# A mean square summed by TensorE, and the first modulation weights loaded in two halves

## The chip, the core and the metric

The kernel runs on one core of a Trainium2 chip. Its time is the device time of one execution in microseconds; before the change the median of three runs is 1152.08 us (1148.12 to 1154.47). The core has five engines with instruction queues of their own: TensorE (PE; its weight loads are listed as PEld), VectorE (DVE), ScalarE (ACT), GpSimd (POOL) and SyncE (SP), which here issues the DMA transfers. Each queue is worked off in order, so an instruction that waits holds up all that stand behind it in its queue.

## The reference, cut to what matters

Two transformer blocks over 512 tokens of width 1024, in float32. The change is at the entry of the first block:

```python
mod = silu(c) @ w_mod + b_mod                     # w_mod: 1024 x 3072
shift, scale, gate = split(mod, 3)
u = x * rsqrt(mean(x*x, axis=-1) + 1e-6) * norm_w * (1 + scale) + shift
p = u @ w_in                                      # and so on: attention, convolution, output
```

## The kernel before, in words

Activations lie transposed: the 1024 features are eight tiles `xs[0..7]` of 128 partitions x 512 tokens. So the mean square of a token is a sum over partitions and tiles, and the factor 1/rms must be the same on all partitions of a column; it is kept as a tile `bs` of 128 x 512 that holds it on every partition.

The first block begins in these steps (`block1`, line 341):

1. SP issues the loads in the order of the program: vectors and a constant, the eight tiles of x, group 0 of `w_mod` (four transfers of 128 x 1024, `mod_load`), two of the eight pieces of `w_start`, group 1 of `w_mod`; the rest as buffers come free (two for `wr`, ten for `modw`).
2. `warm_up` gives TensorE 8 + 20 products of zeros, whose results nobody reads.
3. `norm_bs`: ScalarE squares each tile, VectorE adds the squares up (seven additions), TensorE reduces over partitions with four products by a column of 1/1024, ScalarE takes the root and VectorE the reciprocal of 128 x 4 numbers, TensorE spreads them by four transposes, and ScalarE copies the result into `bs`.
4. `mod_group` multiplies one group of `w_mod` (512 columns) by silu(c): eight products that write 32 partitions each, four of them side by side in the array; ScalarE copies the result from PSUM (`part`); four small products by `sel32` give it in columns (`cols`). `mod_pair` makes shift and scale (`shift`, `A1`) for two feature tiles of it, on VectorE. Groups 0 to 3 serve the tiles 0 to 7, groups 4 and 5 the gate.
5. For each tile j, `apply_mod` makes u: x * bs on VectorE, then scale and shift on ScalarE into a high part, the same into float32, and the low part by a subtraction on VectorE. `w_start[j]` is split the same way into `wh` and `wl`. Then come 18 products (six outputs, three each: high x high, weights x low part, low weights x high): the block of tile j. They accumulate in PSUM over the eight blocks.

One PSUM bank (`pj`) serves the warm-up, the sum of squares and `mod_group` in turn, one (`pv`) the `cols`. The pool `tA` has four buffers. A scheduler puts the instructions of each engine in order when the program is built, from dependencies and its own estimate of times; so instructions of one block may stand among those of another. Behind the eight blocks come the gated products (`glu`), the convolution on VectorE (31 taps for each of four tiles, put off by a low priority), the projections with `w_in`, and q with `w_q` (first piece of it: a tile `wh` too).

Of the kernel before, what the change touches and what calls it, by code (L numbers as in the profile page):

```python
# [16 lines left out]
AF = mybir.ActivationFunctionType  # L17
# [5 lines left out]
P = 128  # L23
S = 512
D = 1024
KT = 8
# [120 lines left out]
def rest(k, src, hi, lo):  # L147
    return k.V.tensor_tensor(out=lo, in0=src, in1=hi.bitcast(F32), op=ALU.subtract)
# [32 lines left out]
def mm3(k, ps, wh, wl, ah, al, first, last):  # L181
    mm = k.T.matmul
    mm(ps, wh, ah, start=first, stop=False)
    mm(ps, wh, al, start=False, stop=False)
    k.mm = mm(ps, wl, ah, start=False, stop=last)
    return k.mm
# [77 lines left out]
def bcast(k, r, n, tag):  # L264
    b = k.t(tag)
    for j in range(n):
        k.T.transpose(b[:, j * P:(j + 1) * P], r[:, j:j + 1].to_broadcast([P, P]), k.ident)
    return b
# [66 lines left out]
MODW = 10  # L335
LATER = 1500
CTX = (0, 2)
WARM = (8, 20, 0)
ZG = (1, 0, 1, 1, 1, 0, 0, 0, 0, 0, 0)

def block1(k, I, st, h1d):
    A, V, T, G, Y = k.A, k.V, k.T, k.G, k.Y
    k.consts("c1", 1408)
    S1 = ExitStack()
    k.open(S1, "S", dict(modw=MODW, bs=1))

# [3 lines left out]
    def warm_up(n):  # L350
        ps = k.t("pj")
        for _ in range(n):
            T.matmul(ps, warm[:, 0:P], warm, start=True, stop=True)

    xs = []
# [8 lines left out]
    cc = k.cal([KT, 32])  # L364
# [2 lines left out]
    A.activation(th[:, 0:1], th[:, 0:1], AF.Sqrt, scale=0.0, bias=k.eps[1e-6])  # L367

    mark = [None] * 3
    warm_up(WARM[0])  # L370
    warm_up(WARM[1])
    shift, A1 = k.cal([2, KT]), k.cal([2, KT])
    gate = k.cal([KT])
    bm1 = k.cal([KT])
# [2 lines left out]
    def mod_load(g, i):  # L377
        t = k.t("modw", [2, S])
        Y.dma_start(out=t, in_=I["w_mod"][g, i])
        return t  # L380

    def mod_group(ts):
        ps = k.t("pj")
        for kt in range(KT):
            q = 32 * (kt % 4)
            T.matmul(ps[q:q + 32, :], cc[:, kt, :], ts[kt // 2][:, kt % 2, :], start=kt < 4, stop=kt >= 4)
        part = k.t("tA")
        A.activation(part, ps, AF.Copy)
        cols = k.t("pv", [4, 2])
        for i in range(4):  # L390
            T.matmul(cols[:, i, :], part[:, i * P:(i + 1) * P], k.sel32[:, 0:2], start=True, stop=True)
        return cols

    def mod_pair(g, ts):
        cols = mod_group(ts)
        for e in range(2):
            j = 2 * g + e
            V.tensor_scalar(out=shift[:, :, j], in0=cols[:, 2 * e, :], scalar1=k.vec("b_mod", j), scalar2=None, op0=ALU.add)
            V.tensor_scalar(out=A1[:, :, j], in0=cols[:, 2 * e + 1, :], scalar1=bm1[:, j:j + 1],
                            scalar2=k.vec("norm_w", j), op0=ALU.add, op1=ALU.mult)  # L400

    def mod_gate(g, ts):
        cols = mod_group(ts)
        V.tensor_tensor(out=gate[:, 4 * g - 16:4 * g - 12], in0=cols[:, :, 0], in1=k.vec("b_mod", 4 * g, 4), op=ALU.add)

    def norm_bs(vals, w, tag):
        ss = SumSq(k, "tA", w)
        for v in vals:
            ss.add(v)
        r = ss.rstd("pj", k.inv1k, 1e-6, k.cal([w // P]))  # L410
        b = bcast(k, r, w // P, "pv")
        bs = k.t(tag, [D] if tag == "modw" else [w])[:, :w]
        mark[1] = A.activation(bs, b[:, :w], AF.Copy)
        return bs

    def apply_mod(x, w, bs, i, j, hi, lo, vec=False):
        t = k.t("tA", [w])
        mark[1] = V.tensor_tensor(out=t, in0=x, in1=bs, op=ALU.mult)
        a_ap, s_ap = A1[:, i, j:j + 1], shift[:, i, j:j + 1]
        A.activation(hi, t, AF.Identity, bias=s_ap, scale=a_ap)  # L420
        if vec:
            V.tensor_scalar(out=t, in0=t, scalar1=a_ap, scalar2=s_ap, op0=ALU.mult, op1=ALU.add)
        else:
            mark[2] = A.activation(t, t, AF.Identity, bias=s_ap, scale=a_ap)
        V.tensor_tensor(out=lo, in0=t, in1=hi.bitcast(F32), op=ALU.subtract)
        return hi, lo

    bs = norm_bs(xs, S, "bs")
    warm_up(WARM[2])
    a0, a1 = k.t("s", [2, S]), k.t("s", [2, S])  # L430
    accs = [a0[:, 0, :], a0[:, 1, :], a1[:, 0, :], a1[:, 1, :], k.t("pt"), k.t("pt")]
    us = []

    mods = [[mod_load(0, i) for i in range(4)]]
    raws = []

    def raw_load(j):
        raw = k.t("wr", [1024])
        Y.dma_start(out=raw[:, :768], in_=I["w_start"][j])
        raws.append(raw)  # L440

    raw_load(0)
    raw_load(1)
    mods.append([mod_load(1, i) for i in range(4)])
    for j in range(KT):
        raw, wh, wl = raws[j], k.t("wh", [1024], F32R), k.t("wl", [1024], F32R)
        A.activation(wh[:, :768], raw[:, :768], AF.Copy)
        if j % 2 == 0:
            mod_pair(j // 2, mods[j // 2])
        u = apply_mod(xs[j], S, bs, 0, j, k.t("U", dt=F32R), k.t("U", dt=F32R))  # L450
        us.append(u)
        rest(k, raw[:, :768], wh[:, :768], wl[:, :768])
        if j + 2 < KT:
            raw_load(j + 2)
        if j % 2 == 0 and j // 2 + 2 < 6:
            mods.append([mod_load(j // 2 + 2, i) for i in range(4)])
        for m in range(6):
            c = slice(m * P, (m + 1) * P)
            mm3(k, accs[m], wh[:, c], wl[:, c], u[0], u[1], j == 0, j == KT - 1)
# [41 lines left out]
    for g in range(4):  # L501
        wh, wl = W1.next()
        for kk in range(2):
            j = 2 * g + kk
            c = slice(kk * S, (kk + 1) * S)
            for t in range(4):
                tt = slice(t * P, (t + 1) * P)
                uh, ul = us[j]
                ps = q_ps[t // 2][:, t % 2, :]
# [18 lines left out]
    for t in (2, 3, 4, 5, 0, 1):  # L528
        ps = k.t("pt", [256])
        for j in range(KT):  # L530
# [3 lines left out]
            o = (t if t < 2 else t - 2) * P  # L534
# [222 lines left out]
    for pr in range(4):  # L757
        for half in range(2):
            i = 2 * pr + half
# [27 lines left out]
    for m in range(KT):  # L787
        ps = k.t(("pj", "pt", "pt", "pv")[m % 4])
# [652 lines left out]
def emit(tc, I, out, dbg=None, stages=("b1", "b2", "ff")):  # L1441
    k = K(tc, dbg)
    nc = tc.nc
    with ExitStack() as st:
        k.open(st, "g", dict(g=1, wr=2, wh=3, wl=2))
        setup(k, I)
        h1d = nc.dram_tensor("h1d", (KT, P, S), F32, kind="Internal").ap()
        k.open(st, "H", dict(xa=6, xb=4, hg=16))
        p1 = ExitStack()
        k.open(p1, "p1", dict(c1=1, U=16, tA=4, kvs=6))  # L1450
        k.open(p1, "p1m", dict(pj=1), PSUM)
        k.open(p1, "p1s", dict(s=2), PSUM)
        k.open(p1, "p1t", dict(pt=2), PSUM)
        k.open(p1, "p1v", dict(pv=1), PSUM)
        if "b1" not in stages:
            k.rest()
        if "b1" in stages:
            nm = block1(k, I, p1, h1d)
        else:
            nm = Norm(k, "norm_mix_g", "hg", "xb")  # L1460
            for j in range(KT):
                x = k.x()
                k.Y.dma_start(out=x, in_=I["xT"][:, j, :])
                k.Y.dma_start(out=h1d[j], in_=x)
                nm.add(j, x)
        p1.close()
        k.nx = 0
        if "b2" in stages:
            k.open(st, "p2a", dict(c2=1, p=6, rk=4, v=2, z=2, bon=3, s8=6, nr=8))
            k.open(st, "p2m", dict(pj=2), PSUM)  # L1470
            k.consts("c2", 1350)
            block2(k, I, nm, h1d, out)
# [94 lines left out]
```

## Time and profile before

| | |
|---|---|
| runs | 1152.08 us median of 3 (1148.12 to 1154.47) |
| profiled execution | 1149.1 us, of which the span is 1147.3 us |
| PE busy | 1084.9 us, 95% |
| DVE busy | 728.2 us, 63% |
| ACT busy | 538.3 us, 47% |
| first matmul of a block of u | 23.32 us |
| last matmul of the eighth block | 72.22 us |
| first matmul of the projection behind them | 78.38 us |

The table's upper part is from the page, its last three rows from the timeline of TensorE. Nearly all instructions are recorded on line 57, a helper, so they are told apart by their tiles: `s<-U,wh` writes the accumulator s from a high part of u (U) and a high part of weights (wh). A product in float32 is recorded as two matmuls, so x16 stands for eight products of `mod_group`; a product of the blocks is recorded as one. The kernel does nothing over and over, so a microsecond at its entry counts once.

### The profile page before, as it was taken

To read this page: it belongs to the slowest core of one execution; us is meant where nothing else is said; L and a number is where in the kernel's file an instruction comes from. 1 tells how busy PE (TensorE), PEld (TensorE's weight loads), DVE (VectorE), ACT (ScalarE), POOL (GpSimd) and SP (SyncE) were. 2 spreads that over 40 slices of the span, in tenths; PEclk is the share of its full clock that TensorE was granted. 3 is DMA by queue.
4 is the path that set the end of the run, shared out by engine and by line. 5 is a ranking of instruction groups with operands and counts; after the bars stand their busy time and mean duration, and the time that the engine had idled before them with its cause. 6 is when DMAs were issued, how large, how long until landed. Compare 5 with 4: busy or idle time off the path is not lost.

```text
span 1147.3 us, 15927 instructions
## 1 busy us (share of the span) xinstructions
PE 1084.9 (95%) x6268; PEld 835.6 (73%) x6268; DVE 728.2 (63%) x1260; ACT 538.3 (47%) x987; POOL 66.9 (6%) x222
## 2 busy tenths in 40 slices
PE   7999989985998899999999898999999999999998
PEld 3668966553686677777768675768888888888887
DVE  3459999986454698888866888657444334334332
ACT  5444546766434366564646575555434133233220
POOL 0000000000001111121111012010000000000000
PEclk8999999997998999999989998999999999999999
DMA  8753221001143211010101221212232233233332
GB/s 304 266 199 96 74 88 38 1 23 32 55 166 105 67 38 56 20 38 19 38 20 52 74 75 37 75 55 84 86 106 92 92 103 99 92 94 107 94 118 85
DMA packets 30603, 96.46 MB, mean 84 GB/s; under 512 B 3392, under 2 KB 4160, under 8 KB 30528
## 3 DMA queue, kind: packets, MB, share of 16 engines
q1 hardware_dynamic: 30528, 95.45, 25.6%
q8 instruction: 49, 0.80, 0.3%
q14 instruction: 26, 0.21, 0.1%
HBM read 91.24 MB, written 4.19 MB: 83 GB/s over the span
## 4 chain that ended last, share of the span: by engine, by line
PE 81%; DVE 7%; ACT 4%; POOL 3%; issue 2%; DMA 2%; SPq 0%; ACTq 0%; DVEq 0%; POOLq 0%
PE pf L57 30%; PE pj L57 23%; PE i L57 7%; PE s L57 7%; PE pt L57 6%; PE pv L57 4%; PE y L57 3%; POOL nr L57 3%; DVE hg L57 2%; ACT p L57 1%; DVE c L57 1%; DVE wl L57 1%; DVE tA L57 1%; ACT wh L57 1%; DMA wr<-w_in 1%
## 5 line engine op out<-in xcount | busy, mean ns | idle before, releaser
L57 ACT ACTIVATE wh<-wr 128x1024 fp32r<-128x1024 f32 (+1 forms) x132 | 137.5, 1042 | 175.7 <-PE pf L57 63.5
L57 DVE TENSOR_TENSOR wl<-wr,wh 128x1024 fp32r<-128x1024 f32 (+1 forms) x132 | 158.6, 1203 | 11.8 <-ACT wh L57 4.5
L57 PE MATMUL pj<-hg,wh 128*128 128x512 f32 x448 | 155.0, 418 | 3.2 <-ACT r L57 1.8
L57 PE MATMUL pf<-A,wh 128*128 128x512 f32 x512 | 157.7, 389 | 0.0
L57 ACT ACTIVATE f<-i 128x512 f16<-128x512 f32 (+1 forms) x132 | 72.0, 597 | 90.6 <-PE i L57 90.5
L57 PEld LDWEIGHTS pf<-A,wh 128*128 128x128 f32 x512 | 96.0, 188 | 19.7
L57 PE MATMUL pf<-A,wl 128*128 128x512 f32 x256 | 99.6, 389 | 0.0
L57 PEld LDWEIGHTS pj<-hg,wh 128*128 128x128 f32 x448 | 81.4, 193 | 20.6 <-issue 2.0
L57 DVE TENSOR_TENSOR x<-x,pf 128x512 f32<-128x512 f32 (+1 forms) x33 | 22.1, 671 | 114.0 <-PE pf L57 114.0
L57 PE MATMUL pj<-hg,wl 128*128 128x512 f32 x224 | 91.0, 406 | 1.5 <-DVE wl L57 1.5
L57 DVE SCALAR_TENSOR_TENSOR hg<-hg,c 128x498 f32<-128x498 f32 (+14 forms) x120 | 84.8, 735 | 0.4
L57 PE MATMUL pf<-ff,wh 128*128 128x512 f32 (+1 forms) x272 | 79.7, 377 | 0.0
L57 PE MATMUL pf<-hg,wh 128*128 128x512 f32 x256 | 78.8, 389 | 0.0
L57 DVE SCALAR_TENSOR_TENSOR fr<-pf,r 128x512 f32<-128x512 f32 x32 | 22.1, 691 | 85.4 <-PE pf L57 82.1
L57 ACT ACTIVATE fr<-fr 128x512 f32<-128x512 f32 x32 | 20.2, 632 | 100.2 <-DVE fr L57 100.2
L57 PEld LDWEIGHTS <-f 128*128 128x128 f16 x720 | 46.0, 100 | 23.6 <-issue 14.3
L57 PE MATMUL i<-f 128*128 128x128 f16 x672 | 55.7, 224 | 5.7 <-DVE f L57 5.3
L57 PEld LDWEIGHTS pf<-ff,wh 128*128 128x128 f32 x272 | 50.1, 188 | 9.4
L57 PE MATMUL pj<-U,wh 128*128 128x512 f32 x160 | 53.3, 410 | 3.4 <-DVE hg L57 3.3
L57 PEld LDWEIGHTS pf<-A,wl 128*128 128x128 f32 x256 | 48.0, 188 | 10.1
L57 PEld LDWEIGHTS pf<-hg,wh 128*128 128x128 f32 x256 | 48.0, 188 | 10.0
L57 PE MATMUL pf<-ff,wl 128*128 128x512 f32 (+1 forms) x136 | 51.2, 376 | 0.0
(302 smaller groups left out, 2123.9 us busy)
## 6 DMA issues: line engine op xcount, KB each, us to landing
wr<-w_ff SPq DMA_DIRECT2D x64, 512.0 KB, 3.5
modw<-w_mod SPq DMA_DIRECT2D x24, 512.0 KB, 7.0
wr<-rw_in SPq DMA_DIRECT2D x20, 512.0 KB, 3.5
wr<-w_out SPq DMA_DIRECT2D x16, 512.0 KB, 3.5
wr<-w_in SPq DMA_DIRECT2D x10, 512.0 KB, 3.5
wr<-w_start SPq DMA_DIRECT2D x8, 384.0 KB, 4.3
x<-xT SPq DMA_DIRECT2D x8, 256.0 KB, 5.2
wr<-w_q SPq DMA_DIRECT2D x4, 512.0 KB, 3.6
```

The lines of the kernel that those rows point to most:

```text
L57: r = f(*a, **kw)
```

## The change

It does two things in `block1`, and sets two constants.

- The sum of squares: a constant 128 x 128 matrix of 1/1024 (`ones`) is multiplied by each square, accumulating over the eight tiles in `pj`. The result is the mean square on every partition. ScalarE takes the root of all 128 x 512 numbers into `bs`, and VectorE the reciprocal of all of them, in place. The seven additions, the four products by a column, the small root and reciprocal, the four transposes and the copy are gone for x; `norm_bs` stays for the context.
- Group 0 of `w_mod` is loaded as two halves of 256 columns (four transfers of 128 x 2 x 256 each), the first before `w_start[0]`, the second between `w_start[0]` and `w_start[1]`. `mod_group` and `mod_pair` take the range of halves, and tile 0 calls the first, tile 1 the second. The other groups stay whole.
- 12 warm-up products in place of 28, and 128 columns more for constants.

```diff
-WARM = (8, 20, 0)
+WARM = 12
...
-    def mod_group(ts):
+    def mod_group(ts, e0=0, e1=2):
         ps = k.t("pj")
+        o = slice(e0 * 256, e1 * 256)
         for kt in range(KT):
             q = 32 * (kt % 4)
-            T.matmul(ps[q:q + 32, :], cc[:, kt, :], ts[kt // 2][:, kt % 2, :], start=kt < 4, stop=kt >= 4)
+            T.matmul(ps[q:q + 32, o], cc[:, kt, :], ts[kt // 2][:, kt % 2, o], start=kt < 4, stop=kt >= 4)
         part = k.t("tA")
-        A.activation(part, ps, AF.Copy)
+        A.activation(part[:, o], ps[:, o], AF.Copy)
         cols = k.t("pv", [4, 2])
-        for i in range(4):
+        for i in range(2 * e0, 2 * e1):
...
-    bs = norm_bs(xs, S, "bs")
-    warm_up(WARM[2])
+    ones = k.cal([P])
+    G.memset(ones, 1.0 / D)
+    ps = k.t("pj")
+    for j in range(KT):
+        sq = k.t("tA")
+        A.activation(sq, xs[j], AF.Square)
+        T.matmul(ps, ones, sq, start=j == 0, stop=j == KT - 1)
+    bs = k.t("bs")
+    A.activation(bs, ps, AF.Sqrt, bias=k.eps[1e-6])
+    V.reciprocal(out=bs, in_=bs)
...
-    mods = [[mod_load(0, i) for i in range(4)]]
+    mods = [[k.t("modw", [2, S]) for i in range(4)]]
+
+    def half_load(e):
+        for i in range(4):
+            Y.dma_start(out=mods[0][i][:, :, e * 256:(e + 1) * 256], in_=I["w_mod"][0, i][:, :, e * 256:(e + 1) * 256])
+    half_load(0)
...
     raw_load(0)
+    half_load(1)
     raw_load(1)
...
-        if j % 2 == 0:
+        if j < 2:
+            mod_pair(0, mods[0], j, j + 1)
+        elif j % 2 == 0:
             mod_pair(j // 2, mods[j // 2])
```

The scheduler also moves instructions, on TensorE at three places. The first is the entry, behind the warm-up; `pj<-modw` are the products of `mod_group`, `pv<-g,tA` its small products, `s` and `pt` the accumulators of the blocks, `c_83` the tile of constants.

```order
-L57 MATMUL pj<-g,tA 128x1 x4
-L57 MATMUL pj<-modw,c_83 32x512
-L57 MATMUL pv<-g,c_83 128x128 x4
-L57 MATMUL pj<-modw,c_83 32x512 x7
-L57 MATMUL pv<-g,tA 128x2 x4
+L57 MATMUL pj<-tA,c_83 128x512 x8
+L57 MATMUL pj<-modw,c_83 32x256 x8
+L57 MATMUL pv<-g,tA 128x2 x2
+L57 MATMUL pj<-modw,c_83 32x256 x8
+L57 MATMUL pv<-g,tA 128x2 x2
 L57 MATMUL s<-U,wh 128x512 x2
 L57 MATMUL pt<-U,wh 128x512 x2
```

Both halves of group 0 stand ahead of the first block, though only tile 1 needs the second. On ScalarE, too, the two copies of `part` stand ahead of the first high part of u.

The second place is TensorE between the blocks of tiles 1 and 2, with groups 1 and 2 of `w_mod`.

```order
 L57 MATMUL pt<-U,wh 128x512 x2
 L57 MATMUL pt<-U,wl 128x512
-L57 MATMUL pj<-modw,c_83 32x512 x6
+L57 MATMUL pj<-modw,c_83 32x512 x4
 L57 MATMUL pv<-g,tA 128x2 x4
-L57 MATMUL pj<-modw,c_83 32x512 x6
+L57 MATMUL pj<-modw,c_83 32x512 x8
 L57 MATMUL s<-U,wh 128x512 x2
 L57 MATMUL pt<-U,wh 128x512 x2
-L57 MATMUL pj<-modw,c_83 32x512 x2
+L57 MATMUL pv<-g,tA 128x2 x4
 L57 MATMUL s<-U,wh 128x512
```

Group 1 was cut into 2 + 6 products and is now cut into 4 + 4; group 2 was 6 + 2 and is whole. Groups 3 and 4 were 5 + 3 each, the latter parts among the first products of tiles 4 and 6; now both are whole and stand between tiles 5 and 6, so that the blocks of tiles 2 to 5 follow one another.

The third place is TensorE behind the block of tile 7, with group 5. First the rows before, then the rows now; `s<-wh,U` are products of q with the first piece of `w_q`, `pj<-U` the first projection.

```order
L57 MATMUL pt<-U,wl 128x512
L57 MATMUL pv<-g,tA 128x2 x4
L57 MATMUL pj<-modw,c_83 32x512 x8
L57 MATMUL pv<-g,tA 128x2 x4
L57 MATMUL pj<-U,wh 128x512 x2
```

```order
L57 MATMUL pt<-U,wl 128x512
L57 MATMUL pv<-g,tA 128x2 x4
L57 MATMUL pj<-modw,c_83 32x512 x8
L57 MATMUL s<-wh,U 128x512 x2
L57 MATMUL pv<-g,tA 128x2 x4
L57 MATMUL pj<-U,wh 128x512 x2
```

Two products of q have come up ahead of the last small products and of the projections; they need the first piece of `w_q`, split by ScalarE. VectorE's queue now has the low part of the first `w_in` piece ahead of the gated products, and the load of `w_q` waits for that. Behind the convolution, about a quarter into the program, the orders before and after are the same.

## Rows read from the trace of the kernel before

**Rows 1.** The page's first part: busy us (share) x instructions of each engine
```profile
PE 1084.9 (95%) x6268; PEld 835.6 (73%) x6268; DVE 728.2 (63%) x1260; ACT 538.3 (47%) x987; POOL 66.9 (6%) x222
```
**Rows 2.** Stretches: length, busy PE, PEld, DVE, ACT, POOL; clock; DMA share, GB/s
```profile
4.70:9.60 4.90, 4.74 (x21) 1.86 (x19) 1.99 (x3) 4.46 (x8) 0.00 (x0) 1.00 0.94 317
9.60:13.00 3.40, 0.00 (x0) 0.02 (x1) 2.85 (x5) 1.85 (x3) 0.00 (x0) 0.80 1.03 413
13.00:15.20 2.20, 1.84 (x8) 1.77 (x8) 0.01 (x1) 0.27 (x1) 0.00 (x0) 0.50 1.02 415
```
**Rows 3.** Timeline of PE, entry: start, us, instruction, [idle before, releaser]
```profile
1.41 8.09 PE L57 MATMUL pj<-bs 128*128 128x512 bf16 x28 [1.41 <-POOL bs L57]
...
15.26 1.89 PE L57 MATMUL pj<-modw,c 128*32 128x512 f32 x2 [0.40 <-issue]
...
18.12 2.06 PE L57 MATMUL pj<-modw,c 128*32 128x512 f32 x14
20.92 1.05 PE L57 MATMUL pv<-g,tA 128*128 128x2 f32 x8 [0.74 <-ACT tA L57]
23.32 0.74 PE L57 MATMUL s<-U,wh 128*128 128x512 f32 x2 [1.35 <-ACT U L57]
...
25.65 0.50 PE L57 MATMUL s<-U,wh 128*128 128x512 f32 x1
```
**Rows 4.** Timeline of ACT, entry
```profile
8.17 3.36 ACT L57 ACTIVATE tA<-x 128x512 f32<-128x512 f32 x5 [0.28 <-DMA x<-xT]
...
20.27 0.60 ACT L57 ACTIVATE tA<-pj 128x512 f32<-128x512 f32 x1 [1.38 <-PE pj L57]
...
22.45 0.81 ACT L57 ACTIVATE U<-tA,c 128x512 fp32r<-128x512 f32 x1 [0.86 <-DVE c L57]
```
**Rows 5.** Timeline of PE, the blocks and behind them
```profile
33.12 1.91 PE L57 MATMUL pj<-modw,c 128*32 128x512 f32 x12
...
51.89 1.06 PE L57 MATMUL pj<-modw,c 128*32 128x512 f32 x6
...
72.22 0.39 PE L57 MATMUL pt<-U,wl 128*128 128x512 f32 x1
73.78 1.05 PE L57 MATMUL pv<-g,tA 128*128 128x2 f32 x8 [1.17 <-ACT tA L57]
...
77.47 1.05 PE L57 MATMUL pv<-g,tA 128*128 128x2 f32 x8 [0.78 <-ACT tA L57]
78.38 0.71 PE L57 MATMUL pj<-U,wh 128*128 128x512 f32 x2
```
**Rows 6.** Stretch behind the blocks, columns as in Rows 2
```profile
78.40:90.00 11.60, 11.60 (x53) 9.64 (x53) 10.85 (x23) 2.40 (x3) 0.00 (x0) 1.00 0.22 73
```
**Rows 7.** Timeline of DVE, entry
```profile
7.40 5.47 DVE L57 TENSOR_TENSOR tA<-tA 128x512 f32<-128x512 f32 x7 [3.77 <-ACT tA L57]
...
18.92 1.29 DVE L57 TENSOR_TENSOR tA<-x,bs 128x512 f32<-128x512 f32 x2 [3.55 <-ACT bs L57]
```
**Rows 8.** Timeline of PE: products of 128 x 512 with a constant matrix in float32
```profile
225.12 2.74 PE L57 MATMUL pj<-hg,c 128*128 128x512 f32 x6
```
**Rows 9.** DVE groups by shape: count | busy us, mean ns | idle before
```profile
L57 DVE RECIPROCAL c<-c 128x8 f32<-128x8 f32 x6 | 1.2, 197 | 3.3 <-ACT AR L57 3.3
...
L57 DVE RECIPROCAL c<-c 128x2 f32<-128x2 f32 x2 | 0.3, 154 | 0.0
```
**Rows 10.** DMA issues between 5.00 and 5.41: count, KB each, us to landing
```profile
x<-xT SPq DMA_DIRECT2D x1, 256.0 KB, 5.9
```
**Rows 11.** Stretches of transfers at the entry, columns as in Rows 2
```profile
2.20:2.60 0.40, 0.40 (x2) 0.15 (x1) 0.00 (x0) 0.00 (x0) 0.00 (x0) 1.00 0.85 234
5.00:6.00 1.00, 0.98 (x5) 0.48 (x5) 0.00 (x0) 0.98 (x2) 0.00 (x0) 1.00 0.91 305
14.00:15.00 1.00, 0.85 (x5) 0.77 (x4) 0.00 (x0) 0.11 (x1) 0.00 (x0) 0.50 1.03 414
```
**Rows 12.** Timeline of ACT: the first piece of w_q
```profile
78.01 1.05 ACT L57 ACTIVATE wh<-wr 128x1024 fp32r<-128x1024 f32 x1
```

More of the change, by code (lines that the diff above doesn't have):

```diff
@@ L342, in block1 @@
     A, V, T, G, Y = k.A, k.V, k.T, k.G, k.Y
-    k.consts("c1", 1408)
+    k.consts("c1", 1536)
     S1 = ExitStack()
@@ L369, in block1 @@
     mark = [None] * 3
-    warm_up(WARM[0])
-    warm_up(WARM[1])
+    warm_up(WARM)
     shift, A1 = k.cal([2, KT]), k.cal([2, KT])
@@ L380, in mod_load, with mod_pair @@
         return t
-    def mod_group(ts):
+    def mod_group(ts, e0=0, e1=2):
         ps = k.t("pj")
+        o = slice(e0 * 256, e1 * 256)
         for kt in range(KT):
             q = 32 * (kt % 4)
-            T.matmul(ps[q:q + 32, :], cc[:, kt, :], ts[kt // 2][:, kt % 2, :], start=kt < 4, stop=kt >= 4)
+            T.matmul(ps[q:q + 32, o], cc[:, kt, :], ts[kt // 2][:, kt % 2, o], start=kt < 4, stop=kt >= 4)
         part = k.t("tA")
-        A.activation(part, ps, AF.Copy)
+        A.activation(part[:, o], ps[:, o], AF.Copy)
         cols = k.t("pv", [4, 2])
-        for i in range(4):
+        for i in range(2 * e0, 2 * e1):
             T.matmul(cols[:, i, :], part[:, i * P:(i + 1) * P], k.sel32[:, 0:2], start=True, stop=True)
         return cols
-    def mod_pair(g, ts):
-        cols = mod_group(ts)
-        for e in range(2):
+    def mod_pair(g, ts, e0=0, e1=2):
+        cols = mod_group(ts, e0, e1)
+        for e in range(e0, e1):
             j = 2 * g + e
```

## The prediction

> **What bounds the kernel now.** The page's first part comes first: TensorE is busy for 1084.9 us of the span, VectorE for 728.2 [rows 1]. So the change is worth what it takes from TensorE's waiting and from TensorE's own work at the entry, and no more. The stretches of the entry are read next, then TensorE's timeline. The reader is to see a hole. The warm-up ends at 9.5 us [rows 3]; until 13.0 TensorE has nothing, because VectorE's seven additions take 5.47 us behind the squares [rows 7]. In that hole the granted clock drops: 1.00 up to 9.60, 0.80 on average up to 13.00, 0.50 after (1.2 instead of 2.4 GHz) [rows 2]. So the first product of group 0, with the transposes queued behind it, runs at the lower clock: 1.89 us for one product, while the seven others then take 2.06 us together [rows 3]. Only after that come the copy of 0.60 us at 20.27, the small products until 21.97, and the first high part of u at 22.45 [rows 3, 4]. The first block starts at 23.32, and its first product with a low part at 25.65 [rows 3]. From there to the last product of the eighth block, at 72.22 [rows 5], TensorE has only short gaps.
>
> **The sum of squares.** Removed from the path: the additions, four column products, the small root and reciprocal, four transposes and the copy. Added: eight products of 128 x 512 by a constant matrix. Three such take 2.74 us elsewhere [rows 8], which is 0.85 us from one to the next and 0.2 us for the last to drain. ScalarE delivers the third square just before 7.9 us and the eighth at 11.53 [rows 4], 0.67 us each, so TensorE is the slower. With twelve warm-up products it is free at about 5.6 (21 of the 28 lie in the 4.90 us from 4.7 on, 0.23 us each; seven or eight came before [rows 2, 3]); by the third square it is at work on the second until 8.2, and six more take it to 13.3, plus the drain 13.5. The pool's four buffers don't slow this: square five needs the first product's buffer, long done. The root of 128 x 512 from PSUM I take as the copy's 0.60 us [rows 4]: 14.1. The reciprocal of 512 columns does not occur. From 2 to 8 columns it grows by 43 ns [rows 9], 7.2 ns a column, so 3.8 us; the floor is a plain pass over 128 x 512, 0.65 us [rows 7]; the ceiling, had those few columns understated the slope by two thirds, is 6.3 us. I take 3.8: `bs` is ready at 17.9, against 18.89 before by the end of its copy (VectorE's first use starts at 18.92 [rows 7]). That alone would win little; what matters is what else is late by then.
>
> **The two halves.** The last tile of x lands at about 11.0 (issued just after 5.0, 5.9 us to landing [rows 10]); transfers keep the order of issue. Group 0's halves come in runs of 1 KB instead of 4 KB. Runs of 4 KB moved at 414 GB/s, the 2 KB runs of x at 305, the first vectors with 1.1 KB at 234 with the engines busy for 0.85 of the time [rows 11]. For 1 KB I take 250 GB/s, near the last. The bounds: 414, if only the start of the program made the earlier rates low; and 200, by a line through the times of a run at 2 and 4 KB (16 engines: 107 and 158 ns, so 82 ns at 1 KB). A half of 1.05 MB takes 4.2 us (2.5 to 5.2). So the first half lands at 15.2, `w_start[0]` 0.95 us later at 16.2, the second half at 20.4, `w_start[1]` at 21.3, and the first two tiles of group 1, 1.27 us each, by 23.9.
>
> Splitting ought to let tile 0 go on with the first half. It can't: TensorE's queue has both halves' products and small products ahead of the first block, and ScalarE's queue both copies ahead of u. So the wait for the second half replaces the one for the products at low clock. From 20.4: 0.5 us for the last products, 0.4 for a copy of half the width (from 0.60 for the whole), 0.8 for the high part of u [rows 4]: the first block starts at 22.3, 1.0 us earlier than before. The reciprocal is hidden by this wait: 17.9, the small additions and 0.65 us for x * bs make 19.0, and 21.4 is early enough. At 6.3 us it would still just be hidden; if the halves are fast, it is what is late. The low part comes behind a cast and an in-place pass on ScalarE (0.8 us each) and a subtraction on VectorE, at about 24.7, 0.9 us earlier than 25.65. Group 1's first four products, which stand before it, are fed at 23.9 and end at 24.4.
>
> The Trainium skill's page "DMA: Bandwidth & Descriptors", under Specifications, gives 512 B as the least transfer that runs at line rate. By it the halves of 1 KB runs would cost nothing extra, which is the first rival below; the rows at 1.1 and 2 KB, both below the rate at 4 KB, speak against it so far.
>
> **The order of the groups.** Four products of `mod_group` run side by side, so it is rounds that count: three products of group 3 took 1.06 us, six of group 1 took 1.91 [rows 5]. A round is 0.95 us, full or not. Before, groups 1 to 4 were cut 2 + 6, 6 + 2, 5 + 3, 5 + 3: one round too many each. Now there is none: minus 3.8 us. Against that, the cuts covered waits. Between tiles 5 and 6 TensorE now waits for the copy of group 3, as it does for the last group (0.78 us [rows 5]), and, as I estimate, 0.2 us each for the high and the low part of u: plus 1.2. Together minus 2.6. The loads are in time for this: group 2 lands at about 32.5 (after 26.4 for group 1, `w_start[2]`, four tiles of 1.27 us), wanted at about 35.
>
> **Behind the blocks.** Before, it takes 6.2 us from the last block product at 72.22 to the first projection product at 78.38 [rows 5]. The same work stands there now and the waits change by about 0.1, but two products of q (0.45 us) are done in the last wait: minus 0.3. From then on TensorE is busy without a gap, and VectorE nearly so, 10.85 of 11.60 us [rows 6]. VectorE's convolution starts as much earlier as the gated products do, so the lead should survive; I take off 0.2 for its changed order.
>
> **The sum.** 0.9 + 2.6 + 0.3 - 0.2 = 3.6 us less: 1149.1 - 3.6 = 1145.5 for an execution like the profiled one (span 1147.3 and 1.8 around it). That one lay 3.0 us below the median of the runs, so against the median: 1152.1 - 3.6 = 1148.5. All times below are against the median.
>
> **The rivals.**
> - Halves at full rate. The second half lands at 17.0; then the reciprocal decides: u starts at 19.0, the first block at 19.9, the first low part at about 22.7. That is 2.9 instead of 0.9: 5.6 us less, 1146.5. For it speaks only that the low rates fell into the program's first microseconds.
> - The clock falls. Between 14 and 22 us TensorE now has short spells of products, each waiting for a transfer. If the clock goes to 0.50 there, as it did in the hole before [rows 2], the last products of the second half cost 0.5 us more and the first 3 us of the block 1.3 more: 1.8 us less gain, 1150.3. Against it: no single wait is as long as that hole of 3.5 us. The Trainium skill's page "TensorE: Matmul & The Clock Gate", under HAM oscillation, describes just this, a clock lost again and again to waits for transfers between short runs of matmuls; the trace has one such fall.
> - The first q products hold up TensorE: slower. Its queue cannot pass them, and they need the split of `w_q`, which ended at 79.06 before [rows 12]. At that time still, the small products and the projection would start 1.4 us after it, at 80.5 instead of 78.4; with 0.45 us of q done, 1.7 us slower: 1153.8. It turns slower than before from about 77.0. Against it: the load of `w_q` waits for the low part of `w_in`, now ahead of the gated products; I have the split done at 71 to 72.
> - The convolution eats the lead. VectorE's queue behind 78 us is ordered anew, and TensorE waits for it later on. If that costs 3.6 us, nothing changes: 1152.1. A luckier order gives as much.
>
> **How the numbers follow.** Forecast 0.46 (its own range 1146.3 to 1151), full rate 0.18, clock 0.16, q 0.10, convolution 0.10. The range goes from the first rival's reach and some luck behind it, 1143, to the third's, 1154; the runs of one kernel spread over 6 us, so it can't be narrower. Half a per cent, 5.8 us, is about what a measurement of this kernel tells from no change. Faster by more (below 1146.3): a quarter of the forecast's cases, half of the first rival's, a third of the last's: 0.25. Slower by more (above 1157.8): only where two mishaps meet, 0.06. The rest, 0.69, is within.
>
> **What would show it.** In the changed profile: eight products `pj<-tA` about 0.85 us apart, ending near 13.4; a reciprocal of 128 x 512 near 3.8 us; `pj<-modw` of the second half ending near 21, released by a transfer and not by VectorE; the first `s<-U` near 22.3; one wait of 0.8 us between tiles 5 and 6; the first `pj<-U` near 75 and no long wait ahead of `s<-wh`. I am wrong if the first block starts before 21 or after 24, if the granted clock is 0.50 at 22 us, or if the lead at 75 us is not there at 190.

## The result and the profile after

The changed kernel takes 1144.24 us (median of 13 runs, 1137.73 to 1147.42) against 1151.17 us before (13 runs beside them, 1147.4 to 1155.24). The ratio of the runs is 0.9938, 95% interval 0.9921 to 0.9955: 7.1 us less, 5.2 to 9.1. So it is a little faster, and the median lies within the forecast's range of 1143 to 1154. But the forecast's 3.6 us lie below that interval, and the prediction gave only 0.25 to a time below 1146.3. The profiled execution took 1144.24 us (span 1142.5); the one before took 1149.1 (span 1147.3).

TensorE's busy time did not move. This is the page's first part after the change, beside [rows 1]:

```profile
PE 1084.6 (95%) x6272; PEld 836.6 (73%) x6272; DVE 726.8 (64%) x1253; ACT 537.5 (47%) x987; POOL 67.6 (6%) x223
```

The engine is busy as long as before and waits 4.5 us less (span less busy time: 62.4 us before, 57.9 now). The entry, in TensorE's timeline (start, us, instruction, [idle before, releaser]), answers to [rows 3]:

```profile
6.86 7.49 PE L57 MATMUL pj<-tA,c 128*128 128x512 f32 x16
15.19 1.07 PE L57 MATMUL pj<-modw,c 128*32 128x256 f32 x16 [0.84 <-ACT bs L57]
16.99 0.69 PE L57 MATMUL pv<-g,tA 128*128 128x2 f32 x4 [0.74 <-ACT tA L57]
17.61 2.29 PE L57 MATMUL pj<-modw,c 128*32 128x256 f32 x16
20.45 1.01 PE L57 MATMUL pv<-g,tA 128*128 128x2 f32 x4 [0.54 <-ACT tA L57]
21.32 1.20 PE L57 MATMUL s<-U,wh 128*128 128x512 f32 x2
...
25.17 0.80 PE L57 MATMUL s<-U,wh 128*128 128x512 f32 x1
```

Compare the first products of a block: 1.20 us here, 0.74 before. The reason stands in the stretches (length, busy time of PE, PEld, DVE, ACT, POOL, granted clock, DMA share, GB/s), which answer to [rows 2]:

```profile
13.00:17.00 4.00, 2.42 (x21) 0.71 (x19) 1.83 (x1) 1.80 (x3) 0.00 (x0) 1.00 1.07 361
17.00:18.00 1.00, 1.00 (x8) 0.79 (x12) 1.00 (x1) 0.00 (x0) 0.00 (x0) 0.69 1.04 392
18.00:20.00 2.00, 1.91 (x16) 0.51 (x8) 2.00 (x5) 0.00 (x0) 0.00 (x0) 0.50 1.03 411
25.00:28.00 3.00, 3.00 (x11) 2.30 (x8) 0.00 (x0) 0.84 (x1) 0.00 (x0) 0.56 1.04 412
```

Before, the clock fell in a hole where TensorE had nothing to do. Here it holds until after 17 and then falls to 0.50 until nearly 28, with the first block inside. The first block is 2.0 us earlier than before, yet the first product with a low part (25.17) only 0.5 us.

Behind it, the order of the groups shows in the same timeline (answers to [rows 5]):

```profile
58.57 1.05 PE L57 MATMUL pv<-g,tA 128*128 128x2 f32 x8 [0.74 <-ACT tA L57]
...
61.88 0.74 PE L57 MATMUL s<-U,wh 128*128 128x512 f32 x2 [0.41 <-ACT U L57]
63.46 0.50 PE L57 MATMUL s<-U,wh 128*128 128x512 f32 x1 [0.36 <-DVE U L57]
...
72.25 1.05 PE L57 MATMUL pv<-g,tA 128*128 128x2 f32 x8 [1.25 <-ACT tA L57]
73.24 1.92 PE L57 MATMUL pj<-modw,c 128*32 128x512 f32 x16
75.09 0.73 PE L57 MATMUL s<-wh,U 128*128 128x512 f32 x2
...
76.85 0.71 PE L57 MATMUL pj<-U,wh 128*128 128x512 f32 x2
```

No group is cut, three waits stand between tiles 5 and 6 (0.74, 0.41, 0.36), and the q products `s<-wh,U` run ahead of the projection, without a wait. At the projection the lead is 1.5 us, and the q products are done besides. That is far from 7.1. Where the rest comes from was the question for the experiments.

### The profile page after: what moved, and what is told of

Same layout as the page of the kernel before. It is cut to its first block, busy times and chain, and to the rows that moved or that the text cites. A ratio compares the mean times of both kernels' runs of the same rounds, so it can differ in the third digit from the quotient of the medians.

```text
span 1142.5 us, 15940 instructions
## 1 busy us (share of the span) xinstructions
PE 1084.6 (95%) x6272; PEld 836.6 (73%) x6272; DVE 726.8 (64%) x1253; ACT 537.5 (47%) x987; POOL 67.6 (6%) x223
## 4 chain that ended last, share of the span: by engine, by line
PE 83%; DVE 5%; ACT 4%; POOL 3%; DMA 2%; issue 2%; SPq 0%; ACTq 0%; POOLq 0%; DVEq 0%
PE pf L57 31%; PE pj L57 23%; PE pt L57 7%; PE i L57 7%; PE s L57 7%; PE pv L57 5%; PE y L57 3%; POOL nr L57 3%; DVE hg L57 1%; ACT p L57 1%; ACT tA L57 1%; DVE c L57 1%; ACT wh L57 1%; DMA x<-xT 1%; DMA wr<-rw_in 1%
## 5 line engine op out<-in xcount | busy, mean ns | idle before, releaser
L57 DVE SCALAR_TENSOR_TENSOR hg<-hg,c 128x499 f32<-128x499 f32 (+14 forms) x120 | 85.0, 739 | 0.8 <-ACT hg L57 0.4
```

Source lines behind the costliest of these rows:

```text
L57: r = f(*a, **kw)
```

## The experiments

Each kernel's ratio is to the kernel before, on the same chip. All times of products below are starts in TensorE's timeline, unless said otherwise.

**The mean square alone** (group 0 loaded and multiplied whole):

```diff
-    mods = [[k.t("modw", [2, S]) for i in range(4)]]   # and both half_load
+    mods = [[mod_load(0, i) for i in range(4)]]
-        if j < 2:
-            mod_pair(0, mods[0], j, j + 1)
-        elif j % 2 == 0:
+        if j % 2 == 0:
```

> The mean square on TensorE alone; group 0 is loaded and multiplied whole. Theory A (the gain comes from the entry and from the order of the groups, which the new mean square brings by itself, since the scheduler then places groups 1 to 4 whole): the square root ends near 15.2 us and the reciprocal near 18.5 as in the changed kernel, group 0's products start near 15.2, the first block comes between 20.0 and 21.5 us, no group is cut by a block, time 0.993 to 0.996 of before. Theory B (the halves are needed, since a whole group 0 arrives late): first block at 22.5 or later, time 0.998 or more of before.

Measured: 1144.4 us, 0.9935 (0.9916 to 0.9955): the whole gain. Its entry in TensorE's timeline:

```profile
14.64 2.89 PE L57 MATMUL pj<-modw,c 128*32 128x512 f32 x16 [0.84 <-ACT bs L57]
18.29 1.05 PE L57 MATMUL pv<-g,tA 128*128 128x2 f32 x8 [0.76 <-ACT tA L57]
21.59 1.22 PE L57 MATMUL s<-U,wh 128*128 128x512 f32 x2 [2.26 <-ACT U L57]
```

The first block is at 21.59, 0.1 past what theory A allowed and well short of theory B's 22.5; the clock fell here too, at 20. Group 1 is still cut, one product ahead of the first low part and seven behind the block; groups 2 to 4 are whole. The 12 warm-up products and the new order belong to this kernel too: no run has the new mean square without them, so their shares of the gain are not told apart.

**The halves alone** (mean square and 28 warm-up products as before):

```diff
-WARM = 12   # and the mean square on TensorE
+WARM = 28
+    bs = norm_bs(xs, S, "bs")
```

> Group 0 in two halves alone; the mean square stays on VectorE and the warm-up has 28 products. Theory A: the additions on VectorE and the fall of the clock behind them stay, the groups are cut by blocks as before; first block 22 to 23.5 us, time 0.998 to 1.001 of before. Theory B (the halves carry the gain): first block before 21.5 us and 0.993 to 0.996.

Measured: 1152.34 us, 0.9997 (0.9977 to 1.0017): no difference that the runs can tell, as theory A had it. The trace shows something more, behind the last block:

```profile
77.19 2.85 PE L57 MATMUL pj<-modw,c 128*32 128x512 f32 x16
80.80 1.87 PE L57 MATMUL pv<-g,tA 128*128 128x2 f32 x8 [0.76 <-ACT tA L57]
82.53 1.20 PE L57 MATMUL pj<-U,wh 128*128 128x512 f32 x2
```

The same instructions with the same waits took 1.92, 1.05 and 0.71 us elsewhere (1.05 and 0.71 in the first trace of before [rows 5], 1.92 in that of the changed kernel, above). Here the clock fell at 78 and stayed at 0.50 for 10 us. So the same waits can come with a fall or without one.

**Whole loads, two products** (only the transfers of group 0 are whole again):

```diff
-    half_load(0)        # and half_load(1) behind raw_load(0)
+    mods = [[mod_load(0, i) for i in range(4)]]
```

> The changed kernel with group 0 loaded whole but still multiplied in two halves; TensorE's order is that of the changed kernel. My prediction's step (halves in runs of 1 KB arrive late and decide the first block) would give a first block 1 us earlier than the changed kernel's 21.3. What the changed kernel's trace shows (the second half waits for no transfer) gives the same first block within 0.4 us and the changed kernel's time within 0.2 per cent: 0.992 to 0.996 of before.

Measured: 1143.74 us, 0.9919 (0.9889 to 0.9949). TensorE's timeline and the stretch from 13 us:

```profile
15.65 0.63 PE L57 MATMUL pj<-modw,c 128*32 128x256 f32 x4 [0.18 <-DMA modw<-w_mod]
16.93 0.63 PE L57 MATMUL pj<-modw,c 128*32 128x256 f32 x4 [0.65 <-DMA modw<-w_mod]
18.64 1.07 PE L57 MATMUL pj<-modw,c 128*32 128x256 f32 x16
21.00 0.73 PE L57 MATMUL s<-U,wh 128*128 128x512 f32 x2
```

```profile
13.00:17.00 4.00, 2.33 (x17) 0.53 (x17) 2.19 (x1) 0.69 (x1) 0.00 (x0) 1.00 1.03 413
```

Now the first half's products wait for transfers (0.18 and 0.65), and the second half's for none. In the changed kernel it is the other way round: there weight loads of the second half waited for transfers, 0.5 us in all in the first trace and 1.0 in the second (in us, times, longest):

```profile
PEld pj L57 <- DMA modw<-w_mod: 1.0, 2, 0.6
```

In the time it comes to the same. The clock held in this trace up to 71 us, though: the changed kernel's first block comes at 21.32 where the clock fell, as expected, but at 20.38 and 20.55 in the two later traces where it held, about 0.5 us ahead of the 21.00 here. In this stretch whole tiles moved at 413 GB/s, halves at 361 (first fence of stretches above), both with the 3 KB runs of `w_start[0]` between them. The changed kernel's second trace has a stretch with hardly anything but halves:

```profile
15.00:16.00 1.00, 0.97 (x16) 0.31 (x16) 1.00 (x1) 0.50 (x1) 0.00 (x0) 1.00 1.09 348
```

My 250 was far too low. The Trainium skill's page "DMA: Bandwidth & Descriptors", Specifications, which counts any transfer of 512 B or more as line rate, is nearer: by these rows 1 KB runs lose an eighth to a sixth.

**Two products that keep TensorE busy:**

```diff
+            last[0] = k.after(T.matmul(a1[:, 1, :w], ones, xs[0][:, :w], start=True, stop=True), last[0])
...
     V.reciprocal(out=bs, in_=bs)
+    filler(1, 512)   # and one behind the products of the first half
```

> The changed kernel with two more products of 128 x 512 in float32 that nobody reads, one behind the eight products of the mean square and one behind the first half of group 0, so that TensorE has no wait over 0.3 us between 12 and 18 us. Theory C (the granted clock falls at 17.4 us because TensorE stood still for short waits, and the fall costs 3 us in the blocks): clock 1.00 from 15 to 28 us, first block at 20.2 to 20.6, first low part near 23, first product of the projection 2 to 3 us earlier than 76.85, time 0.9910 to 0.9925 of before. Rival (the fall costs nothing because ScalarE and VectorE set the pace there): clock 1.00 but the first product of the projection within 0.7 us of 76.85 and 0.993 to 0.996. If the clock falls all the same, theory C's cause is wrong.

Measured: 1140.64 us, 0.9897 (0.9864 to 0.993). The clock is 1.00 from 9 to 28, and this is the timeline:

```profile
13.79 1.02 PE L57 MATMUL s<-x,c 128*128 128x512 f32 x2
...
15.79 1.13 PE L57 MATMUL s<-x,c 128*128 128x512 f32 x2
...
20.11 0.73 PE L57 MATMUL s<-U,wh 128*128 128x512 f32 x2
```

The trace did what theory C said: the first block came at 20.11, the first projection product came at 74.72, 2.1 us earlier than in the changed kernel's first trace, although the clock fell at 70 this time. But run again beside the changed kernel, the advantage was gone:

> The changed kernel with the two unread products again, beside the changed kernel on the same chip. Theory C: clock 1.00 from 12 to 28 us again, first block at 20.0 to 20.4 us; the median 1.5 to 4 us under the changed kernel's, since the fall near 17 us hits only some executions of the changed kernel (one of the two traces), and costs 3 us there. Rival (the first comparison was luck): medians within 1 us of each other.

> The changed kernel, unchanged, as the partner of the kernel with two unread products: 0.992 to 0.9955 of before. Its first block at 20.3 to 20.5 us where the clock holds, 21.3 where it falls near 17 us; from the first block to the last block product 46.8 to 47.1 us where no fall lies between, against 48.9 before.

Measured side by side: 1143.02 us, 0.9943 (0.9925 to 0.9962) with the two products, 1141.89 us, 0.9944 (0.992 to 0.9967) without. So the two products are worth nothing that these runs can tell. Whether a held clock at the entry is worth something they don't show: both profiled executions here held it (first block at 20.19 with the products, 20.55 without). No version was found that beats the changed kernel measurably. The profiled execution with the two products took 1152.86 us this time, against 1142.01 in its first trace: the same program. The first had 41 us at the low clock, the second 68 us, at places such as 71 to 81, 535 to 542 and 703 to 713. Followed product by product, the second is within 0.1 us of the first up to 70 us, 3.1 us late at 80, 5.2 at 580, 8.4 at 600 and 10.8 from 720 on; its lateness changes where one of the two is at the low clock, and by 0.3 us at most elsewhere. So 27 us more at the low clock made 10.9 us.

**Mean square alone with four such products:**

> The mean square alone, group 0 loaded and multiplied whole, with four products that nobody reads (one behind the mean square's, one behind group 0's, two behind its small products), so that TensorE has no long wait before the first block. Theory: without the fall at 20 us that the mean square alone had, first block at 20.6 to 21.3, time 0.989 to 0.993 of before, and as good as the halves with two such products within 1.5 us. If the halves have a worth of their own once the clock holds: 2 us or more slower than that kernel.

Measured: 1142.87 us, 0.9944 (0.9923 to 0.9965). The clock held at the entry, and the first block is later than expected:

```profile
21.53 0.73 PE L57 MATMUL s<-U,wh 128*128 128x512 f32 x2 [0.44 <-ACT U L57]
```

The time is 0.2 us from that of the halves with two such products, measured beside it, though the ratio is above what was expected; the halves are worth nothing here that the runs can tell either. In the traces where the clock held, the halves bring the first block 1.0 to 1.4 us ahead of this one, but the last block product (67.95 here) only 0.4 to 0.8 us (67.52 in the third trace of the changed kernel, 67.11 with the two products).

**Both kernels again, for second traces:**

> The kernel before, unchanged, for a second trace. Theory C (the changed part gives 2 to 2.5 us, and the rest of the 7.1 us is falls of the granted clock, which hit the kernel before more in a typical execution than in the one that was profiled): the span follows the mean granted clock by about 0.9 us for each 0.001, and this execution, near 1150 to 1153 us, shows low-clock stretches that the first trace did not have, one of them between 77 and 90 us, with 2 us or more lost there. Rival (the changed part itself gives more than its 2 us, at places with the same clock): the stretches are those of the first trace, at 12, 264, 360 and 589 us, and the time is within 1 us of its 1149.1.

> The changed kernel, unchanged, for a second trace beside the second one of before. Theory C: median 0.992 to 0.9955 of before; the fall of the clock near 17 us is there again, since the waits that lead to it are the same in every execution; what comes behind 100 us may differ. First block 20.2 to 21.6 us. If there is no fall near 17 us, chance decides there too, and first block is then at 20.3 to 21.0 with the first product of the projection near 74 instead of 76.85.

Measured: before 1.0 (0.998 to 1.0021), changed 0.9938 (0.9915 to 0.996). The second trace of before (1148.94 us) was nearly a copy of the first, so the expected fall between 77 and 90 was not seen: for before, a point for the rival. In the second trace of the changed kernel the clock held at 17:

```profile
14.90 1.07 PE L57 MATMUL pj<-modw,c 128*32 128x256 f32 x16 [0.84 <-ACT bs L57]
17.20 1.94 PE L57 MATMUL pj<-modw,c 128*32 128x256 f32 x16
...
20.38 0.73 PE L57 MATMUL s<-U,wh 128*128 128x512 f32 x2
23.03 0.50 PE L57 MATMUL s<-U,wh 128*128 128x512 f32 x1
...
69.03 1.20 PE L57 MATMUL pv<-g,tA 128*128 128x2 f32 x8 [1.25 <-ACT tA L57]
70.16 3.41 PE L57 MATMUL pj<-modw,c 128*32 128x512 f32 x16
...
75.27 0.72 PE L57 MATMUL pj<-U,wh 128*128 128x512 f32 x2
```

The first block is at 20.38, the last block product at 67.40. That is 4.8 us before [rows 5]. Then the clock falls at 70, where it had held in the first trace: the last group takes 3.41 us instead of 1.92, and the lead shrinks to 3.1. The third trace has the same (20.55, 67.52, a fall at 71).

**The order of the groups alone, in the kernel before:**

```diff
-        if j % 2 == 0:
-            mod_pair(j // 2, mods[j // 2])
+        if j == 2:                        # and group 0 at j == 0
+            mod_pair(1, mods[1])
+            mod_pair(2, mods[2])
+        if j == 6:
+            mod_pair(3, mods[3])
+            mod_gate(4, mods[4])          # behind the blocks, group 5 alone is left
```

> The kernel before with the order of the groups alone: groups 1 to 4 are asked for at other tiles, so that groups 2 and 4 stand whole, groups 1 and 3 still cut; mean square and entry unchanged. My prediction's term (0.95 us for each round saved, less the waits): two rounds fewer, 1.9 us, less about 1 us of waits, 0.9985 to 1.0 of before. If the uncut groups carry the gain of the changed kernel: 0.994 to 0.997. If the waits decide: over 1.000.

Measured: 1156.51 us, 1.0041 (1.0023 to 1.006): slower. Its waits among the blocks:

```profile
39.80 1.05 PE L57 MATMUL pv<-g,tA 128*128 128x2 f32 x8 [0.74 <-ACT tA L57]
...
43.74 0.50 PE L57 MATMUL s<-U,wh 128*128 128x512 f32 x1 [0.87 <-DVE U L57]
...
62.03 1.05 PE L57 MATMUL pv<-g,tA 128*128 128x2 f32 x8 [0.73 <-ACT tA L57]
65.65 1.05 PE L57 MATMUL pv<-g,tA 128*128 128x2 f32 x8 [0.72 <-ACT tA L57]
```

Whole groups one behind the other leave nothing to cover the copies. From the first block (23.70) to the projection (79.91) it takes 56.2 us against 55.1. Saved rounds count only where other products stand in the copy's wait. That is 1.1 us; most of the 0.4% (4.7 us) lies elsewhere: the mean granted clock of its runs is 0.9738, against 0.9786 for before on this chip, and at 1.0 us per 0.001 (below) that goes with 4.8 us.

**Warm-up products that fill the hole, in the kernel before:**

```diff
-WARM = (8, 20, 0)
+WARM = (8, 36, 0)
```

> The kernel before with 16 more warm-up products, which fill TensorE's hole between 9.5 and 13 us. Theory C: the clock stays 1.00 up to 15 us, the first product of group 0 takes 1 us instead of 1.9, first block at 21.8 to 22.6 instead of 23.32, and 1 to 1.5 us are gained: 0.9985 to 0.999 of before; if the clock then also falls later (near 17 to 20 us), nothing. If the hole is the main cost of the entry: 0.997 or less. If the warm-up holds back the column products behind it, the first block comes at 23.5 or later and the time is over 1.000.

Measured: 1146.45 us, 0.9963 (0.9941 to 0.9985), so more than expected, and 4.3 us by the ratio. But its trace shows no gain at the entry: the clock fell at 16 and 23, and the first block came at 23.29, like before. This execution itself took 1149.16 us, no less than the 1149.1 of before, so the gain of the median is not in it; what it shows is how the falls move. Apart from the warm-up its instructions are those of before in the same order on every engine, so four of them can be followed through both traces. The kernel before:

```profile
222.50 0.65 PE L57 MATMUL pv<-xb,kvs 128*64 128x256 f32 x4 [0.31 <-ACT xb L57]
357.98 0.65 PE L57 MATMUL pj<-g 128*128 128x128 f32 x4 [0.57 <-DVE g L57]
412.99 0.61 PE L57 MATMUL i<-f 128*128 128x128 f16 x8 [0.71 <-DVE f L57]
626.42 0.38 PE L57 MATMUL pj<-wh,hg 128*128 128x256 f32 x1 [0.77 <-ACT p L57]
```

With the longer warm-up:

```profile
227.25 0.65 PE L57 MATMUL pv<-xb,kvs 128*64 128x256 f32 x4 [0.31 <-ACT xb L57]
362.99 0.65 PE L57 MATMUL pj<-g 128*128 128x128 f32 x4 [0.57 <-DVE g L57]
416.02 0.61 PE L57 MATMUL i<-f 128*128 128x128 f16 x8 [0.70 <-DVE f L57]
626.25 0.38 PE L57 MATMUL pj<-wh,hg 128*128 128x256 f32 x1 [0.77 <-ACT p L57]
```

It is 4.75 us late at the first of them and 5.0 at the second, 3.0 at the third, and 0.2 early at the fourth. Nothing was done for that. Before spent 7 us at the low clock from 360 and 7 us from 589, both in stretches where TensorE had work; this execution spent none there, only 3 us at 391. The stretches (columns as in [rows 2]) of before, then with the longer warm-up:

```profile
355.00:375.00 20.00, 17.66 (x72) 14.26 (x71) 6.12 (x10) 8.18 (x11) 0.52 (x4) 0.83 0.35 118
584.00:600.00 16.00, 15.50 (x111) 11.12 (x110) 8.39 (x19) 5.29 (x15) 3.37 (x14) 0.79 0.11 34
```

```profile
355.00:375.00 20.00, 16.80 (x78) 13.84 (x79) 9.51 (x14) 10.95 (x14) 5.18 (x11) 1.00 0.46 146
584.00:600.00 16.00, 15.50 (x129) 11.37 (x130) 11.20 (x22) 6.88 (x18) 3.37 (x14) 1.00 0.12 34
```

## Why the prediction fell short

The direction came out and the median lies in the range, but the sum of 3.6 us was too small: the entry gave more than its term of 0.9, and some of the gain has no term in the sum at all. The same instructions in all traces of the two kernels (start in us; the last two rows are the time of the execution and, within its span, the time at the low clock):

| | before | before, 2nd | changed | changed, 2nd | changed, 3rd |
|---|---|---|---|---|---|
| first block | 23.32 | 22.98 | 21.32 | 20.38 | 20.55 |
| last block product | 72.22 | 71.88 | 70.62 | 67.40 | 67.52 |
| first `pj<-U` | 78.38 | 78.04 | 76.85 | 75.27 | 75.05 |
| `pv<-xb,kvs` | 222.50 | 222.28 | 221.00 | 221.04 | 219.36 |
| `pj<-g` | 357.98 | 357.72 | 355.57 | 356.67 | 353.93 |
| `i<-f` | 412.99 | 412.65 | 408.39 | 409.67 | 407.59 |
| `pj<-wh,hg` | 626.42 | 626.15 | 621.50 | 622.83 | 619.10 |
| execution | 1149.1 | 1148.9 | 1144.2 | 1145.6 | 1141.7 |
| low clock | 47.8 | 44.4 | 47.8 | 47.8 | 41.9 |

- **Sum of squares: right, a little early.** In the first trace the warm-up ended at 6.71 instead of 5.6 and the products at 14.35 instead of 13.5, the root takes 0.69 us instead of 0.60, and the reciprocal, for which there was no row, 3.35 instead of 3.8. It ends at 18.52 (forecast 17.9). VectorE's row:

```profile
15.17 3.35 DVE L57 RECIPROCAL bs<-bs 128x512 f32<-128x512 f32 x1 [11.49 <-ACT bs L57]
```

- **The two halves: the step that failed.** "For 1 KB I take 250 GB/s" gave a second half at 20.4, a first block at 22.3, 1.0 us earlier, and at the first low part the 0.9 us of the sum. The mechanism held: weight loads of the second half waited for transfers, and ScalarE's copy of that half is what the first high part of u follows. The rate did not: the halves moved at 348 to 361 GB/s. With the clock at 1.00 the second half's products end at 19.1 to 19.3, the first block comes at 20.4 to 20.6, 2.4 to 2.9 us earlier, and the first low part at 23.03 and 23.19, 2.1 to 2.6 us earlier. So the term of 0.9 is less than half of what the entry gives where the clock holds, and more than the 0.5 where it falls. Nor is that gain owed to the halves: the mean square alone takes the same time. The first rival had the first block nearly right (19.9), though the second half still decides it and not the reciprocal. I gave it 0.18 since I put the low rates of [rows 11] down to the length of the runs; 348 to 361 GB/s at 1 KB show that length explains little of them. By its own signs the prediction was wrong in each trace: the clock was 0.50 at 22 us in the first, and the first block came before 21 us in the other two.
- **The clock.** The second rival came true as well, in one of three traces of the changed kernel and in the mean square alone: the clock fell without a wait as long as the hole of before (in the changed kernel the longest from 7 us on was 0.84 us), and took back most of the lead at the first low part. I gave it 0.16 beside the others, as if only one could happen. The other two traces have these waits too, and one of 0.64 and 0.43 us more near 8 us, and held the clock. The section of the Trainium skill that the prediction cites, HAM oscillation, tells of long waits for transfers; the fall at the entry of before came in a wait for VectorE instead. Nearer is another section of the Trainium skill's "TensorE: Matmul & The Clock Gate", A second HAM failure mode: psum-queue depth-cycling, where short idle spells between groups of matmuls make the clock go up and down; one of the three traces agrees with it.
- **The order of the groups: right, a little large.** From the first block to the last block product it takes 48.9 us before, 47.0 in the second and third traces of the changed kernel: 1.9 instead of 2.6. The estimated waits between tiles 5 and 6 were 1.2 in the sum and measured 1.5. Part of the order by itself (groups 2 and 4 whole), put into the kernel before, made it slower: the term holds for this order, not for "fewer rounds".
- **Behind the blocks: right where the clock holds.** 6.23 us against 6.16, with 0.45 us of q done in it; the third rival (q holding up TensorE) did not happen. In two of three traces a fall at 70 or 71 costs 1.3 to 1.6 us more.
- **VectorE's new order: right.** From 100 to 222 us nothing is lost but 0.5 to 2 us where the clock falls near 155. In the second trace that is half of the lead (3.1 us at the projection, 1.5 at 222 us).
- **What the sum did not have.** With the clock held, the changed part gives 4.8 us up to the last block product, by the first trace of before. Behind the convolution the instructions are the same, and there the lead changes where one of the two traces is at the low clock, and by 0.6 us at most elsewhere. Both traces of before have the falls near 360 and 589, of 7 us each; none of the three of the changed kernel has the long one near 360, and one of them has only 3 us near 583. Between `pj<-g` and `i<-f` the first two traces of the changed kernel gain 2.0 to 2.2 us on before in this way: in the first the lead goes from 2.4 to 6.0 us where before is at the low clock, and back to 4.6 where the changed kernel falls at 383, for 3 us. The prediction reasons for none of this; what it adds to the gain is luck. The changed part's own worth can be read from executions that spent the same 47.8 us at the low clock: the first two of the changed kernel took 4.9 and 3.5 us less than the first of before.

Over all runs the same can be read from each run's mean granted clock. In 73 runs of before it is 0.9783 on average and in 30 of the changed kernel 0.9802; the span grows by 1.0 and 0.85 us per 0.001 that the clock is lower. Straight lines through the runs give 1148.5 and 1143.0 us at a clock of 0.979. So 5.5 us of the gain stand at equal clock, somewhat above the 3.5 to 4.9 of these traces, and 1.5 to 2 go with fewer falls. Such lines are no proof of cause, but the two traces of the kernel with two unread products, 27 us at the low clock and 10.9 us apart, give 0.40 us for each, and the lines 0.37 to 0.44 (0.001 of the mean clock is 2.3 us at half speed).

What stays open is why a fall comes in one execution and not in another. It is not the waits alone: the same waits stand at 70 and 360 in traces with and without a fall. A shift of the same code by some microseconds goes with other falls, as the warm-up showed, but I have no run that sets the shift by itself, with nothing else changed. So I can't say whether the 1.5 to 2 us would survive another edit at the entry.

## What to carry to other kernels

When a kernel keeps TensorE 95% busy, list the low-clock stretches of at least two traces before weighing an edit of a few microseconds: here one program varied by 10.9 us through them, more than the change is worth. A step that looks like three edits should be tried one at a time: the mean square alone gave all of the gain, the halves none that the runs can tell. Rates read in a program's first microseconds don't price transfers later on, and saved rounds of products count only if other products cover the copies between them.

## What the hardware showed that was not expected

- A reciprocal of 128 x 512 in float32 on VectorE takes 3.35 us, about five times a plain pass of that size (0.68 us for x * bs).
- Halves, in runs of 1 KB, moved at 348 GB/s by themselves and at 361 with runs of 3 KB between them, against 413 for whole tiles (4 KB) in the same place; at 2 to 6 us of the program, 1.1 and 2 KB moved at 234 and 305 [rows 11].
- Sixteen more warm-up products in the kernel before, a one-number edit, made it 0.37% faster (0.9963, 0.9941 to 0.9985), though the trace shows the entry no earlier: its mean clock over the runs was 0.9827, against 0.9786 for before on the same chip.
